# Conformer on one core: weight loads interleaved with modulation vectors, the last three tiles' first taps as diagonal-weight products, and norm roots formed on all partitions

## The chip, the cores and the metric

The kernel runs on 1 core of one Trainium2 chip. The metric is device time in microseconds (us) of one launch; the kernel before took 2624.41 us, the median of 3 runs (2624.28 to 2628.53). The engines are called as the profile calls them: PE does matrix products (PEld its weight loads), DVE vector work, ACT activations and casts, POOL small vector work, and SP issues most of the transfers.

## The reference

The network is a trunk of two layers on one sequence of 256 positions and 2048 channels, all in f32. Layer 0 mixes tokens by a causal Conformer convolution, layer 1 by a Mamba-2 mixer, and each mixer is followed by a squared-ReLU MLP of width 8192. A conditioning vector `c` gives shift, scale and gate vectors for every sub-layer.

```python
sc = jax.nn.silu(c)
mod = (sc @ w_mod[i] + b_mod[i])[:, None, :]
sh1, sc1, g1, sh2, sc2, g2 = jnp.split(mod, 6, axis=-1)
u = rmsnorm(h, norm_mix_g[i]) * (1 + sc1) + sh1
# layer 0: the Conformer convolution
v = u @ w_pw1 + b_pw1
a, gt = jnp.split(v, 2, axis=-1)
v = a * jax.nn.sigmoid(gt)
v = causal_dwconv(v, w_dw, b_dw)            # 31 taps per channel
v = jax.nn.silu(layernorm(v, ln_g, ln_b))
h = h + g1 * (v @ w_pw2 + b_pw2)
u = rmsnorm(h, norm_mlp_g[i]) * (1 + sc2) + sh2
h = h + g2 * sq_relu_mlp(u, w1, w2)
```

The change touches layer 0 up to its MLP, and the root of the norms ahead of both MLPs.

## The kernel before, in words

**Layout.** Activations lie transposed: channels on the 128 partitions, 256 positions along the free axis. The 2048 channels are 16 tiles, in four groups g of four tiles; `h[g]` is one group of the residual.

**Modulation vectors.** One `w_mod` slice of 1 MB gives 128 entries of a vector. A slice is loaded whole and reduced either by DVE (`gemv`, line 255: a product with the broadcast silu(c) in `scb`, summed along the row) or, for the groups in `PE_GROUPS`, by four PE products (line 245), with four more PE products per group (line 269) that turn the row into a column. SC1, SH1 and G1 are scale, shift and gate of the mixer; SC2, SH2 and G2 those of the MLP.

**Transfers.** Every slice and every weight tile is issued on SP's queue, in the order in which the program asks for them (`stream`, line 301): a transfer that waits for its buffer holds all that follow. Weight tiles `w` of 1 MB have three buffers, vectors have two of the kind `wm` and four of the kind `hid`, taken in the ring wm, hid, hid (`self.rings`).

**Opening of layer 0.** The square of `h` is summed tile by tile on DVE (`square_sum`), and the root is formed on two columns and spread back over all partitions (`rstd_cols`, lines 446 to 450, then `spread`, lines 459 and 460). Then the first three 256-column blocks of `w_pw1` (`FIRST = 3`) are multiplied group by group, as each group of the normalised `u` becomes ready (`native`, `vectors`; products on line 591): group g needs its eight vectors SC1 and SH1. SP's order is eight vectors, three weight tiles, eight vectors, three weight tiles, and so on. Group 3 is split into two halves.

**Blocks 3 to 7.** Each remaining block has 16 product instructions per group. Under them ACT makes 24 of the 31 depthwise taps of each channel tile (line 531), DVE the other seven and the additions (lines 539 to 558). `pump` mixes vectors for later stages (the jobs of `EARLY`, then of `LATER`) into the blocks at rates given by tables: `RATE_PW1` inside the blocks, `BETWEEN` before and after the LayerNorm, `RATE_PW2` within the second pointwise product.

**LayerNorm and pw2.** After block 7 come the rest of the pumped vectors, the moments of tiles 0 to 11 (lines 571 and 634), the sums of the last four tiles (line 643), the mean and variance chain (lines 646 to 652), normalisation, silu (line 665), and the split of the result into a high and a low part (lines 427 and 428). Then pw2 runs as fp32r products (line 325) of weights that ACT rounds to a high part `wh` (line 316) and DVE subtracts to a low part `wl` (line 317).

**MLP of layer 0.** The norm root comes again through `rstd_cols` and `spread`. For each group, DVE and ACT form `nrm` (line 478) and the high and low part of `u` (lines 430 and 431), while PE multiplies the first blocks of `w1`. Vectors SC2 and SH2 of the MLP that were not pumped earlier come here as `gemv` on DVE.

Of the kernel before, what the change touches and what calls it, by code (L numbers as in the profile page):

```python
# [15 lines left out]
P = 128  # L16
T = 256
D = 2048
# [21 lines left out]
AHEAD_GLU, AHEAD_CHAIN = 40, 400  # L40
# [6 lines left out]
RATE_PW1 = spread(12, 20)  # L47
BETWEEN = 8, 4
RATE_PW2 = spread(16, 16)
# [5 lines left out]
OPEN = 3  # L55
ACT_TAPS = 24

# [3 lines left out]
PE_GROUPS = {(0, G1, g) for g in range(4)} | {(0, SC2, 0), (0, SH2, 0)}  # L61
# [26 lines left out]
def layout(inp):  # L88
# [26 lines left out]
    for l, s, g in PE_GROUPS:  # L115
        cols = wm[l, :, s, 4 * g:4 * g + 4].reshape(4, 4, P, 512)
        wmt[l, s, 4 * g:4 * g + 4] = cols.transpose(0, 2, 1, 3).reshape(4, P, D)
    return {
        "fg": np.ascontiguousarray(a["final_norm_g"].reshape(1, D)),
# [28 lines left out]
class Trunk:  # L148
# [41 lines left out]
    def prologue(self):  # L190
# [12 lines left out]
        for i in range(4):  # L203
            ps = self.bank(self.mm, "mm")
            nc.tensor.matmul(ps, lhsT=self.ones[:1, :], rhs=row[:, i * 512:(i + 1) * 512], start=True, stop=True)
            nc.scalar.activation(out=scb[:, i * 512:(i + 1) * 512], in_=ps, func=AF.Silu)
# [7 lines left out]
                                compare_op=ALU.is_ge, fill=NEG, base=0, channel_multiplier=-1)  # L214
        self.sel = self.t("bT", [P, T], bufs=1)[:, :P]
# [3 lines left out]
        self.eps = self.const("eps", [P, 1])  # L219
        nc.gpsimd.memset(self.eps, EPS)  # L220
# [215 lines left out]
    def rstd_bcast(self, sums, n):  # L436

        return self.spread(self.rstd_cols(sums, n))
# [46 lines left out]
    def conformer(self):  # L485
        nc, a = self.nc, self.a
        ss = []
        for g in range(4):
            for t in range(4):
                ss = self.square_sum(ss, self.h[g][:, t, :])  # L490
        r = self.t("t2", [P, T], bufs=3)
        nc.scalar.copy(out=r, in_=self.rstd_bcast(ss, D))
# [10 lines left out]
        def vectors(g, t0, t1):  # L503

            for t in range(t0, t1):
                self.gemv(0, SC1, 4 * g + t, halves=g == 3)
                self.gemv(0, SH1, 4 * g + t, halves=g == 3)
# [17 lines left out]
        def conv(ct):  # L525

            vp = vpad[ct % 12]

            def products(p4, k):
                for q in range(4):  # L530
                    nc.scalar.activation(out=p4[:, q, :], in_=vp[:, k + q:k + q + T], func=AF.Identity,  # L531
                                         scale=self.col("w_dw", ct * TAPS + k + q),
                                         bias=self.col("b_dw", ct) if k + q == 0 else 0.0)
# [3 lines left out]
            wide = products(four("wh"), 0)  # L537
# [600 lines left out]
```

## Time and profile before

| | us |
|---|---|
| median of the timed runs | 2624.41 |
| profiled execution, its own time | 2629.66 |
| its span | 2627.8 |
| PE busy in the span | 2528.1 (96%) |
| first product of pw1 (line 591) | 42.79 |
| last product of pw1 | 309.70 |
| last sum of the LayerNorm's moments (line 643) ends | 341.37 |
| first silu (line 665) | 348.41 |
| first product of pw2 (line 325) | 349.85 |
| first product of the MLP of layer 0 | 455.44 |

The timeline gives for each row the start and the length in us, the engine, the line, the operation, the tiles written and read, and in brackets the idle time before it with what ended it. A matmul in f32 (lines 591, 643) leaves two records per instruction. The windows view gives, for stretches of the span, the busy time of each engine with its number of instructions, then the granted PE clock as a share of full speed, the DMA share and the GB/s moved.

### The profile page before, as it was taken

The page shows a single profiled execution, that of the slowest core. Times are in us where ns is not written, and L with a number is a line of the kernel's source. Part 1 is how long each engine was busy: PE and PEld are TensorE (multiplying, and loading weights), DVE is VectorE, ACT ScalarE, POOL GpSimd, SP SyncE. Part 2 cuts the span into 40 slices and gives each one's busy share as a digit, 9 for nine tenths or more (in the row PEclk, how much of TensorE's full clock was granted, in tenths as well). Part 3 has the DMA queues.
Part 4 walks back from the last instruction along what each step waited for, and adds up shares of the span by engine and source line. Part 5 has one row for each costly group of instructions (what it writes and reads, how often), then busy time and mean ns, then how long its engine had stood idle before and what let it go on. Part 6 is the DMA issues. An engine that isn't in the chain of part 4 may idle for free.

```text
span 2627.8 us, 37071 instructions
## 1 busy us (share of the span) xinstructions
PE 2528.1 (96%) x14561; PEld 2188.6 (83%) x14561; DVE 1993.5 (76%) x2663; ACT 1370.0 (52%) x2176; POOL 136.0 (5%) x178
## 2 busy tenths in 40 slices
PE   5889979999999999999999999999999999999998
PEld 3777679988888888888888888888998888888886
DVE  6579798987888889888877777988865565565565
ACT  2089864544444434446777666744444344443443
POOL 1000000000000000000000000000000101101000
PEclk9989989999999999999999999999999999999999
DMA  9855778888888888875555555688665555555554
GB/s 377 358 202 208 312 288 346 314 317 314 306 332 325 319 310 329 306 286 200 188 191 175 178 181 188 238 294 315 238 223 189 193 185 193 192 187 195 183 189 144
DMA packets 92593, 657.43 MB, mean 250 GB/s; under 512 B 10465, under 2 KB 10465, under 8 KB 14465
## 3 DMA queue, kind: packets, MB, share of 16 engines
q1 hardware_dynamic: 88274, 640.73, 66.5%
q0 software_dynamic: 3136, 10.59, 1.4%
q10 hardware_dynamic: 1008, 3.75, 0.4%
q8 instruction: 114, 1.87, 0.3%
q14 instruction: 61, 0.50, 0.1%
HBM read 652.83 MB, written 2.20 MB: 249 GB/s over the span
## 4 chain that ended last, share of the span: by engine, by line
PE 91%; DVE 3%; DMA 3%; ACT 1%; issue 1%; POOL 0%; ACTq 0%; SPq 0%; DVEq 0%
PE mm L325 66%; PE mm L591 8%; PE mm L377 4%; PE mm L376 4%; PE mm L375 4%; DMA hid<-wmT 2%; DVE wl L317 1%; PE mm L245 1%; PE ms L1052 0%; DVE wm L255 0%; PE ms L446 0%; ACT acc L665 0%; PE ms L460 0%; DMA h<-xT 0%; PE ms L1021 0%
## 5 line engine op out<-in xcount | busy, mean ns | idle before, releaser
L325 PE MATMUL mm<-u,wh 128*128 128x512 f32 (+1 forms) x4544 | 1371.8, 364 | 6.8 <-ACT u L427 3.0
L316 ACT CAST wh<-w 128x1024 fp32r<-128x1024 f32 x768 | 806.3, 1051 | 996.3 <-PE mm L325 740.2
L317 DVE TENSOR_TENSOR wl<-w,wh 128x1024 fp32r<-128x1024 f32 x768 | 941.1, 1229 | 454.2 <-ACT wh L316 451.1
L325 PE MATMUL mm<-u,wl 128*128 128x256 f32 x3840 | 1078.6, 282 | 2.1 <-DVE wl L317 2.0
L325 PEld LDWEIGHTS mm<-u,wh 128*128 128x128 f32 x4544 | 812.3, 190 | 148.7 <-issue 3.4
L325 PEld LDWEIGHTS mm<-u,wl 128*128 128x128 f32 x3840 | 730.3, 190 | 7.5 <-DVE wl L317 3.5
L325 PE MATMUL mm<-hid,wh 128*128 128x512 f32 (+1 forms) x1344 | 449.0, 384 | 2.8 <-DVE acc L724 2.8
L325 PE MATMUL mm<-hid,wl 128*128 128x256 f32 x1280 | 358.2, 280 | 0.0
L255 DVE SCALAR_TENSOR_TENSOR wm<-wm,scb 128x2048 f32<-128x2048 f32 x129 | 294.7, 2285 | 2.1 <-DMA wm<-wmT 2.0
L325 PEld LDWEIGHTS mm<-hid,wh 128*128 128x128 f32 x1344 | 247.7, 188 | 56.0 <-DVE acc L724 3.2
L591 PE MATMUL mm<-u,w 128*128 128x256 f32 x1024 | 233.0, 389 | 20.7 <-ACT u L513 20.7
L591 PEld LDWEIGHTS mm<-u,w 128*128 128x128 f32 x1024 | 198.6, 195 | 58.4 <-ACT u L513 21.8
L325 PEld LDWEIGHTS mm<-hid,wl 128*128 128x128 f32 x1280 | 241.9, 189 | 0.4 <-issue 0.2
L377 PE MATMUL mm<-wh,hid 128*128 128x512 f32 x512 | 199.9, 390 | 0.0
L375 PE MATMUL mm<-wh,hid 128*128 128x512 f32 x512 | 199.9, 390 | 0.0
L376 PE MATMUL mm<-wl,hid 128*128 128x512 f32 x512 | 199.5, 390 | 0.0
L531 ACT ACTIVATE taps<-u,par 128x256 f32<-128x256 f32 x384 | 158.2, 502 | 0.6 <-DVE u L522 0.6
L255 DVE SCALAR_TENSOR_TENSOR hid<-hid,scb 128x2048 f32<-128x2048 f32 x39 | 89.1, 2287 | 40.6 <-DMA hid<-wmT 29.7
L377 PEld LDWEIGHTS mm<-wh,hid 128*128 128x128 f32 x512 | 96.1, 188 | 19.7
L375 PEld LDWEIGHTS mm<-wh,hid 128*128 128x128 f32 x512 | 96.2, 188 | 19.6
L376 PEld LDWEIGHTS mm<-wl,hid 128*128 128x128 f32 x512 | 96.1, 188 | 19.6
L278 POOL TENSOR_TENSOR mod<-mod,par 128x4 f32<-128x4 f32 (+1 forms) x50 | 41.0, 821 | 1360.0 <-DVE wm L255 964.0
(209 smaller groups left out, 1586.8 us busy)
## 6 DMA issues: line engine op xcount, KB each, us to landing
w<-w SPq DMA_DIRECT2D x256, 1024.0 KB, 4.9
wm<-wmT SPq DMA_DIRECT2D x137, 1024.0 KB, 7.1
w<-win SPq DMA_DIRECT2D x80, 1024.0 KB, 4.9
hid<-wmT SPq DMA_DIRECT2D x55, 1024.0 KB, 9.6
w<-pw SPq DMA_DIRECT2D x48, 1024.0 KB, 5.0
w<-wout SPq DMA_DIRECT2D x32, 1024.0 KB, 6.8
acc<-ac_d POOLq DMA_DIRECT2D x16, 512.0 KB, 6.7
h<-xT ACTq DMA_DIRECT2D x4, 512.0 KB, 12.8
```

The source lines that it names most:

```text
L245: self.pe = nc.tensor.matmul(self.row_sums[32 * t:32 * t + 32, :], lhsT=self.scol[:, kt:kt + 1].broadcast_to([P, 32]), rhs=w[:, t * 512:(t ...
L255: nc.vector.scalar_tensor_tensor(out=w, in0=w, scalar=1.0, in1=self.scb, op0=ALU.mult, op1=ALU.mult, accum_out=m[:, i:i + 1])
L278: nc.gpsimd.tensor_tensor(out=m, in0=m, in1=self.col("b_mod", (layer * 6 + seg) * NT + 4 * kg + i0, n), op=ALU.add)
L316: nc.scalar.copy(out=wh, in_=w[:, s, :])
L317: nc.vector.tensor_tensor(out=wl, in0=w[:, s, :], in1=wh.bitcast(F32), op=ALU.subtract)
L325: self.pe = self.nc.tensor.matmul(out, lhsT=lhsT, rhs=rhs, skip_group_check=True, **kw).ins
L375: mm(banks[q], lhsT=hi, rhs=wh[:, k, :], start=g == 0 and t == 0, stop=False)
L376: mm(banks[q], lhsT=hi, rhs=wl[:, k, :], start=False, stop=False)
L377: mm(banks[q], lhsT=lo, rhs=wh[:, k, :], start=False, stop=g == 3 and t == 3)
L531: nc.scalar.activation(out=p4[:, q, :], in_=vp[:, k + q:k + q + T], func=AF.Identity, scale=self.col("w_dw", ct * TAPS + k + q), bias=self ...
L591: self.pe = nc.tensor.matmul(o, lhsT=w[:, t, j * P:(j + 1) * P], rhs=u[g][:, t, :], start=g == 0 and t == 0 and j < 2, stop=g == 3 and t == 3,
```

## The change

In the opening, the vector `c` is loaded broadcast to all partitions and put through silu there, `h` comes through SP's queue, and the vectors of the next group are asked for between the three weight tiles of the group before. Squares of `h` are no longer added on DVE: sixteen PE products with a matrix of ones sum them. `rstd_bcast` does the same for the norms of both MLPs, and takes the root and its reciprocal on a 128x256 tile.

`PE_GROUPS` loses the first group of SH2, so that four vectors go from PE to DVE. The rates change: eight instead of twelve vectors in the blocks of pw1, four and six instead of eight and four around the LayerNorm, and a front-loaded `RATE_PW2`.

For the last three channel tiles, the first fifteen of the 31 taps become PE products with diagonal weight matrices, which the host lays out (`diag`, 0.98 MB a tile); ACT makes twelve taps and DVE four. The diagonal matrices lie in three of the `hid` buffers, and from block 7 to the LayerNorm chain vectors use the two `wm` buffers alone. The convolution of the last tile is asked for after the first pumped vectors behind block 7. Normalisation of groups 1 to 3 behind the LayerNorm gets a lower priority than that of group 0.

```diff
-RATE_PW1 = spread(12, 20)
-BETWEEN = 8, 4
-RATE_PW2 = spread(16, 16)
+RATE_PW1 = spread(8, 20)
+BETWEEN = 4, 6
+RATE_PW2 = [2, 1, 1, 1] + spread(13, 12)
+DIAG, PE_TAPS, FEW_TAPS = 3, 15, 12
-PE_GROUPS = {(0, G1, g) for g in range(4)} | {(0, SC2, 0), (0, SH2, 0)}
+PE_GROUPS = {(0, G1, g) for g in range(4)} | {(0, SC2, 0)}
...
-        row = self.b("wm", [1, D], bufs=2)
-        nc.sync.dma_start(out=row, in_=a["crow"])
+        nc.sync.dma_start(out=scb, in_=a["crow"].broadcast_to([P, D]))
-            nc.scalar.dma_start(out=self.h[g], in_=a["xT"][g])
+            nc.sync.dma_start(out=self.h[g], in_=a["xT"][g])
...
     def rstd_bcast(self, sums, n):
-        return self.spread(self.rstd_cols(sums, n))
+        nc = self.nc
+        ps = self.bank(self.ms, "ms")[:, :T]
+        for i, s in enumerate(sums):
+            nc.tensor.matmul(ps, lhsT=self.ones, rhs=s, start=i == 0, stop=i == len(sums) - 1)
+        r = self.t("t2", [P, T], bufs=3)
+        nc.scalar.activation(out=r, in_=ps, func=AF.Sqrt, scale=1.0 / n, bias=self.eps)
+        nc.vector.reciprocal(r, r)
+        return r
...
         for g in range(4):
+            sq = self.b("acc", [P, 4, T], bufs=5)
             for t in range(4):
-                ss = self.square_sum(ss, self.h[g][:, t, :])
-        r = self.t("t2", [P, T], bufs=3)
-        nc.scalar.copy(out=r, in_=self.rstd_bcast(ss, D))
+                nc.scalar.activation(out=sq[:, t, :], in_=self.h[g][:, t, :], func=AF.Square)
+                ss.append(sq[:, t, :])
+        r = self.rstd_bcast(ss, D)
...
+            few = ct >= NT - DIAG
+            k0, k1 = (PE_TAPS, PE_TAPS + FEW_TAPS) if few else (0, ACT_TAPS)
...
+            if few:
+                i = ct - (NT - DIAG)
+                part = (self.bank(self.mm, "mm") if i else self.bank(self.ms, "ms"))[:, :T]
+                with self.tc.issue_after(self.pe):
+                    for k in range(PE_TAPS):
+                        nc.tensor.matmul(part, lhsT=diag[i][:, k, :], rhs=vp[:, k:k + T], start=k == 0,
+                                         stop=k == PE_TAPS - 1)
...
+            if few:
+                nc.vector.tensor_add(wide[:, 0, :], part, wide[:, 0, :])
...
+            vec = lambda n: [self.gemv(0, s, 4 * n[0] + n[1], halves=n[0] == 3) for s in (SC1, SH1)]
+            for t in range(4):
+                vec((0, t))
+            vectors(0, 0, 4)
+            for g in range(3):
+                for i in range(3):
+                    load(i, g)
+                    products(i, g, 0, 4)
+                    if i < 2:
+                        vec((g + 1, i))
+                if g < 2:
+                    for t in (2, 3):
+                        vec((g + 1, t))
+                    vectors(g + 1, 0, 4)
+            vectors(3, 0, 2)
+            for i in range(3):
+                if i:
+                    vec((3, 1 + i))
+                load(i, 3)
+                products(i, 3, 0, 2)
+            vectors(3, 2, 4)
+            for i in range(3):
+                products(i, 3, 2, 4)
...
+            if b == 7:
+                self.rings = ("wm",)
+                diag = []
+                for i in range(DIAG):
+                    diag.append(self.b("hid", [P, PE_TAPS, P]))
+                    self.stream(diag[i], a["diag"][i])
             native([b], glu, pump=pump)
...
         self.pump(BETWEEN[0])
+        close(ct, conv(ct))
+        ct += 1
...
-            for g in range(4):
+        for g in range(4):
+            with self.tc.high_priority(AHEAD_CHAIN if g == 0 else AHEAD_NORM):
...
+        self.rings = ("wm", "hid", "hid")
         with self.tc.issue_after(self.pe):
             self.pump(BETWEEN[1])
```

SP's queue in the opening, from the last of the eight vectors of group 0 on (`hid`, `wm` are vectors, `w` weight tiles); before:

```order
L301 DMA hid_236<-wmT 128x2048
L301 DMA w_58_252<-pw 128x2048
L301 DMA w_59_254<-pw 128x2048
L301 DMA w_60_256<-pw 128x2048
L301 DMA wm_306<-wmT 128x2048
L301 DMA hid_310<-wmT 128x2048
L301 DMA hid_314<-wmT 128x2048
L301 DMA wm_317<-wmT 128x2048
L301 DMA hid_320<-wmT 128x2048
L301 DMA hid_323<-wmT 128x2048
L301 DMA wm_326<-wmT 128x2048
L301 DMA hid_332<-wmT 128x2048
```

and with the change:

```order
L307 DMA hid_203<-wmT 128x2048
L307 DMA w_38_219<-pw 128x2048
L307 DMA wm_237<-wmT 128x2048
L307 DMA hid_241<-wmT 128x2048
L307 DMA w_41_245<-pw 128x2048
L307 DMA hid_263<-wmT 128x2048
L307 DMA wm_266<-wmT 128x2048
L307 DMA w_44_269<-pw 128x2048
L307 DMA hid_287<-wmT 128x2048
L307 DMA hid_290<-wmT 128x2048
L307 DMA wm_293<-wmT 128x2048
L307 DMA hid_299<-wmT 128x2048
```

Two vectors now stand behind the first tile, two behind the second, and four behind the third.

PE behind the last products of block 7 (the first rows; line 245 there is 251 with the change, 643 is 692), before:

```order
L591 MATMUL mm_1640<-u_187,w_260_1707 128x256 x8
L245 MATMUL mm_1751<-wm_1748,scol 32x512 x4
...
L245 MATMUL mm_1751<-wm_1768,scol 32x512 x4
L269 MATMUL mm_1776<-bT_114,t_262_1715 128x1 x4
...
L245 MATMUL mm_1786<-wm_1797,scol 32x512 x4
L245 MATMUL mm_1786<-hid_1803,scol 32x512 x4
...
L571 MATMUL ms_1378<-acc_202,ones 32x256 x4
...
L634 MATMUL mm_1828<-t_281_1826,bT_114 128x512
...
L643 MATMUL mm_1828<-nrm_1969,ones 128x256
L245 MATMUL mm_2057<-hid_2054,scol 32x512 x4
...
L269 MATMUL mm_2082<-bT_114,t_279_1809 128x1 x4
L325 MATMUL mm_2097<-u_1988,wh_2107 128x256
```

and with the change (line 555 is a diagonal-weight product, `hid` its matrices):

```order
L611 MATMUL mm_1584<-u_154,w_236_1645 128x256 x8
...
L251 MATMUL mm_1689<-wm_1700,scol 32x512 x4
L251 MATMUL mm_1689<-wm_1706,scol 32x512 x4
L275 MATMUL mm_1714<-bT_105,t_238_1653 128x1 x4
L555 MATMUL ms_1721<-u_151,hid_1577 128x256 x15
...
L683 MATMUL mm_1774<-t_255_1772,bT_105 128x512
...
L555 MATMUL mm_1776<-u_151,hid_1579 128x256 x15
L555 MATMUL mm_1819<-u_152,hid_1581 128x256 x5
...
L555 MATMUL mm_1819<-u_152,hid_1581 128x256 x10
...
L692 MATMUL mm_1774<-nrm_1860,ones 128x256
L251 MATMUL mm_1948<-wm_1945,scol 32x512 x4
...
L331 MATMUL mm_2000<-u_1879,wh_2027 128x256 x2
```

Four vectors stay ahead of the moments, eight go behind the last sums, and 45 diagonal-weight products stand between them.

DVE in the opening of the MLP of layer 0, ahead of the low parts of the last group of `u` (line 431, 437 with the change), before:

```order
L478 SCALAR_TENSOR_TENSOR nrm_3819<-h_78,mod_3232,ms_3199 128x256
L478 SCALAR_TENSOR_TENSOR nrm_3823<-h_78,mod_3232,ms_3199 128x256
L317 TENSOR_TENSOR wl_3763<-w_525_3756,wh_3762 128x1024
L317 TENSOR_TENSOR wl_3767<-w_525_3756,wh_3766 128x1024
L255 SCALAR_TENSOR_TENSOR wm_3758,mod_3760<-wm_3758,scb 128x2048
L431 SCALAR_TENSOR_TENSOR u_3818<-nrm_3819,mod_3497,u_3818 128x256
L431 SCALAR_TENSOR_TENSOR u_3818<-nrm_3823,mod_3497,u_3818 128x256
L478 SCALAR_TENSOR_TENSOR nrm_3827<-h_78,mod_3232,ms_3199 128x256
L478 SCALAR_TENSOR_TENSOR nrm_3831<-h_78,mod_3232,ms_3199 128x256
```

and with the change:

```order
L491 SCALAR_TENSOR_TENSOR nrm_3745<-h_78,mod_3411,t_422_3117 128x256
L491 SCALAR_TENSOR_TENSOR nrm_3749<-h_78,mod_3411,t_422_3117 128x256
L323 TENSOR_TENSOR wl_3679<-w_493_3672,wh_3678 128x1024
L323 TENSOR_TENSOR wl_3683<-w_493_3672,wh_3682 128x1024
L261 SCALAR_TENSOR_TENSOR hid_3674,mod_3676<-hid_3674,scb 128x2048
L261 SCALAR_TENSOR_TENSOR wm_3734,mod_3676<-wm_3734,scb 128x2048
L261 SCALAR_TENSOR_TENSOR hid_3737,mod_3676<-hid_3737,scb 128x2048
L261 SCALAR_TENSOR_TENSOR hid_3740,mod_3676<-hid_3740,scb 128x2048
L437 SCALAR_TENSOR_TENSOR u_3744<-nrm_3745,mod_3676,u_3744 128x256
L437 SCALAR_TENSOR_TENSOR u_3744<-nrm_3749,mod_3676,u_3744 128x256
L491 SCALAR_TENSOR_TENSOR nrm_3753<-h_78,mod_3411,t_422_3117 128x256
L491 SCALAR_TENSOR_TENSOR nrm_3757<-h_78,mod_3411,t_422_3117 128x256
```

Where one vector (`scb` as a factor) stood between the group's `nrm` and `u`, four stand now; the `nrm` of the other two tiles follows in both.

More of the change, by code (lines that the diff above doesn't have):

```diff
@@ L197, in prologue @@
         nc.gpsimd.memset(self.ones, 1.0)
-        row = self.b("wm", [1, D], bufs=2)
-        nc.sync.dma_start(out=row, in_=a["crow"])
+        nc.sync.dma_start(out=scb, in_=a["crow"].broadcast_to([P, D]))
         nc.scalar.dma_start(out=self.par, in_=a["par"])
         for g in range(4):
-            nc.scalar.dma_start(out=self.h[g], in_=a["xT"][g])
[L203 to L206, printed above, removed]
+            nc.sync.dma_start(out=self.h[g], in_=a["xT"][g])
+        for i in range(2):
+            v = scb[:, i * 1024:(i + 1) * 1024]
+            nc.scalar.activation(out=v, in_=v, func=AF.Silu)
         self.scol = self.const("scol", [P, NT])
```

49 lines of the change are left out of this document (22 added, 27 removed).

## The prediction

> **What bounds the kernel now.** I read the page's busy times and chain first.
>
> ```profile
> PE 2528.1 (96%) x14561; PEld 2188.6 (83%) x14561; DVE 1993.5 (76%) x2663; ACT 1370.0 (52%) x2176; POOL 136.0 (5%) x178
> PE 91%; DVE 3%; DMA 3%; ACT 1%; issue 1%; POOL 0%; ACTq 0%; SPq 0%; DVEq 0%
> ```
>
> PE sets the end. So a change pays where it shortens the time in which PE idles or takes work from PE, and costs where it gives PE work or makes it wait. The timeline of PE shows where it idled (number and cause in brackets):
>
> ```profile
> 42.79 43.46 PE L591 MATMUL mm<-u,w 128*128 128x256 f32 x192 [1.67 <-ACT u L513]
> 94.96 34.31 PE L591 MATMUL mm<-u,w 128*128 128x256 f32 x144 [8.71 <-ACT u L513]
> 139.58 20.37 PE L591 MATMUL mm<-u,w 128*128 128x256 f32 x80 [10.32 <-ACT u L513]
> 319.69 1.94 PE L245 MATMUL mm<-hid,scol 128*32 128x512 f32 x8 [2.66 <-DMA hid<-wmT]
> 339.29 1.22 PE L643 MATMUL mm<-acc,ones 128*128 128x256 f32 x2 [7.77 <-DVE acc L558]
> 349.85 0.78 PE L325 MATMUL mm<-u,wh 128*128 128x256 f32 x3 [2.95 <-ACT u L427]
> ```
>
> There are two places: the opening, up to 152.95 (the last 80 records end at 159.95 and hold 32 of block 3, 7.0 us), and the tail from the last product of pw1 at 309.70 to the full pace of pw2. In the opening ACT's `u` waits for the last vector of its group, so I looked at what the transfers did, in the windows view, and why SP held them, in the waits of SP's queue over the first 160 us:
>
> ```profile
> 0.00:10.00 10.00, 6.86 (x8) 2.49 (x8) 0.00 (x0) 3.07 (x4) 3.02 (x32) 1.00 0.83 322
> 10.00:20.00 10.00, 0.30 (x1) 0.00 (x0) 8.31 (x10) 4.96 (x12) 0.00 (x0) 1.00 1.02 419
> 40.00:50.00 10.00, 8.33 (x29) 6.91 (x30) 8.15 (x10) 2.19 (x5) 0.00 (x0) 1.00 1.02 423
> 60.00:70.00 10.00, 10.00 (x48) 8.81 (x47) 3.98 (x6) 1.82 (x4) 0.20 (x1) 1.00 0.57 215
> 110.00:120.00 10.00, 10.00 (x48) 8.81 (x47) 2.90 (x4) 0.91 (x2) 0.20 (x1) 1.00 0.34 111
> ...
> SPq L301 <- PE mm L591: 85.6, 12, 24.6
> ```
>
> The transfers run full to 50 us, then twice fall to a half and a third, because three weight tiles stand in a row and each needs a buffer that PE still reads; the vectors behind them are held too.
>
> **The change part by part.** *Opening.* With the weight tiles spread, a tile's buffer is asked for only after two more vectors, so SP waits less. Up to the last of the 32 vectors pass 1.05 MB of broadcast `c`, 0.6 MB of parameters, 2.1 MB of `h`, 33.6 MB of vectors and 11 tiles of 1.05 MB, 48.8 MB. The first 10 us carry 3.2 MB; the other 45.6 MB at 0.422 MB/us (between 419 and 423 GB/s) take 108 us, to 118.0. The last vector then needs its landing, two gemvs, whose duration is this row, POOL's addition and `u`:
>
> ```profile
> L255 DVE SCALAR_TENSOR_TENSOR wm<-wm,scb 128x2048 f32<-128x2048 f32 x129 | 294.7, 2285 | 2.1 <-DMA wm<-wmT 2.0
> 302.62 7.15 PE L591 MATMUL mm<-u,w 128*128 128x256 f32 x32
> 309.70 1.06 PE L245 MATMUL mm<-wm,scol 128*32 128x512 f32 x8
> 313.27 1.05 PE L269 MATMUL mm<-bT,t 128*128 128x1 f32 x8
> ```
>
> That is 5.7 us in all, 123.7. Four half groups of products remain (the third tile of group 3 is now loaded last): 16 instructions take 7.0 us, so 14.0, end 137.7. Twice PE's group 2 gives a buffer of `w` free hardly ahead of its tile, for which I add 1.2: end at 139.0 instead of 152.95, **-14.0**. Bounds: -15.2 without that wait, and nothing if SP is held as often as before (second rival). The sixteen square sums move to PE before 42.79, where it has nothing else.
>
> *Blocks 3 to 7.* Four gemvs fewer (four instructions, 0.97 to the next start: 3.9) and one conversion of columns (0.98): **-4.9**. The bound below is nothing, if ACT or DVE set the pace; I take the full sum since each loses taps (36 by ACT, 9 by DVE), and the third rival prices the other. Block 7 thus ends at 309.7 - 18.9 = 290.8.
>
> *Tail.* Times from the end of block 7, with rows of the tail of before, in order of time:
>
> ```profile
> 310.83 0.33 SPq L301 DMA_DIRECT2D wm<-wmT  x1
> 316.00 1.04 PE L245 MATMUL mm<-wm,scol 128*32 128x512 f32 x8
> 326.00 2.07 PE L634 MATMUL mm<-t,bT 128*128 128x512 f32 x2 [0.71 <-ACT t L631]
> 340.31 1.06 PE L643 MATMUL mm<-nrm,ones 128*128 128x256 f32 x2
> 343.96 1.03 ACT L316 CAST wh<-w 128x1024 fp32r<-128x1024 f32 x1
> 347.12 1.28 ACT L665 ACT_TABLE_LOAD   x1
> 348.41 1.09 ACT L665 ACTIVATE acc<-acc,par 128x256 f32<-128x256 f32 x2
> 360.60 0.70 ACT L427 CAST u<-acc 128x256 fp32r<-128x256 f32 x2
> 361.20 2.94 ACT L316 CAST wh<-w 128x1024 fp32r<-128x1024 f32 x3
> 368.33 0.28 PE L325 MATMUL mm<-u,wl 128*128 128x256 f32 x1
> ```
>
> Before, the last sums end at 341.4 (+31.7), the first silu stands at +38.7, the last split at +51.5, and pw2 runs at full pace from 368.15 (+58.45). With the change the four vectors behind block 7 share two buffers, so the third and fourth are issued when PE has used the first and second, and a transfer issued at 310.83 was used at 316.00, 5.2 later: PE waits, and the gemvs and columns end at about +12.8. Then the diagonal products: 15 instructions of 128x256 in f32 are 6.56 us by the 7.0 for 16, 19.7 for the three tiles. With the moments, the spread of 2.07 and the sums (about 0.9 each) between and behind them, the last sum ends at +41.8, 10.1 later. PE's waits of 2.66 and 7.77 are gone, but its own work fills more than their place. Then eight gemvs instead of four, their copies, and two casts stand ahead of the silus: first silu at +52.6, 10.8 behind the sums against 7.0. And SP holds all pw2 weights behind vectors whose `hid` buffers the diagonal products release, so that only one tile is cast ahead of the silus, where before more were (the row at 343.96 is one); from the first silu to full pace 22.8 against 19.75. Sum: 10.1 + 3.8 + 3.0, **+17**. Bounds: +10, if the casts and copies fit between, and +21, if PE goes at half clock, which the windows show after a wait:
>
> ```profile
> 94.90:101.00 6.10, 6.04 (x14) 4.89 (x15) 0.88 (x2) 1.31 (x4) 0.00 (x0) 0.50 1.01 415
> 101.00:107.00 6.00, 6.00 (x29) 5.26 (x29) 4.95 (x5) 0.00 (x0) 0.00 (x0) 1.00 1.01 421
> ```
>
> After 8.71 us of waiting the clock is 0.50 for 6.1 us and half the products pass. I put this cold stretch in the +12.8, in gemvs and columns, and take the diagonal products at full speed, since nothing they need is late. The Trainium skill (TensorE: Matmul & The Clock Gate, Part 1) says that full clock returns after one busy window of 3.4 us and is lost after one idle window of that length; the two rows show a longer return. By the page's figure the tail would come out shorter by an estimated 1 us.
>
> *Opening of the MLP of layer 0.* The four vectors of SH2 that left PE come to DVE, three of them ahead of the last group of `u`. The window up to the first product of group 3 (432 records make three groups) and DVE's rows:
>
> ```profile
> 455.00:509.50 54.50, 53.96 (x434) 53.67 (x435) 0.96 0.84 318
> 503.56 2.29 DVE L255 SCALAR_TENSOR_TENSOR wm<-wm,scb 128x2048 f32<-128x2048 f32 x1
> 505.77 0.88 DVE L431 SCALAR_TENSOR_TENSOR u<-nrm,mod,u 128x256 fp32r<-128x256 f32 x2
> 509.62 0.87 DVE L431 SCALAR_TENSOR_TENSOR u<-nrm,mod,u 128x256 fp32r<-128x256 f32 x2
> ```
>
> PE takes the first low part at 509.5; the first two stand at 506.6 and the other two at 510.5, needed half a block of products later (54.5 / 18 = 3.0), at 512.5. Three gemvs of 2.29 make both 6.9 later: 6.9 less a slack of 2.0, **+4.9**. Bounds: nothing, if DVE waits enough before to take it up, and 6.9 without slack.
>
> *Norm roots.* Before, ACT's root and from there DVE and PE up to `nrm`:
>
> ```profile
> 452.13 0.26 ACT L449 ACTIVATE rcol<-ms,eps 128x2 f32<-128x2 f32 x1
> 454.30 0.87 DVE L478 SCALAR_TENSOR_TENSOR nrm<-h,mod,ms 128x256 f32<-128x256 f32 x2 [1.19 <-PE ms L460]
> 343.54 0.51 ACT L651 ACTIVATE a<-a,eps 128x256 f32<-128x256 f32 x1 [1.28 <-DVE a L650]
> 344.89 1.75 DVE L652 RECIPROCAL a<-a 128x256 f32<-128x256 f32 x1
> ```
>
> From 452.13 to 454.30 is 2.17; the LayerNorm's rows give 0.51 + 1.75 = 2.26 on 256 columns. Three roots: **+0.5**, with the handovers.
>
> Sum: -14.0 - 4.9 + 17 + 4.9 + 0.5 = +3.5 on the profiled execution's own 2629.66 us, 2633.2. That execution lies 5.2 us above the median of the runs, so 2628.
>
> **The rivals.** *The tail is cheaper (2618).* The waits overlap: copies, casts and the eight gemvs run while DVE and ACT do the LayerNorm chain, the tail costs +10, and the gemvs in the MLP's opening cost 2 because DVE's waits there take them up. Then -14.0 - 4.9 + 10 + 2 + 0.5 = -6.4 and 2618. For it: before, PE idles 2.95 ahead of pw2, so ACT and not PE sets that place. Against it: the order of the copies and casts on ACT, ahead of the first silu.
>
> *The opening doesn't fill (2642).* The change doesn't do what it says: SP still stands at a `w` buffer. At the mean of the stretch from 10 to 130 us before,
>
> ```profile
> 10.00:130.00 120.00, 81.16 (x349) 69.76 (x348) 77.52 (x91) 16.57 (x37) 5.54 (x16) 0.96 0.91 371
> ```
>
> 45.6 MB end at 133, the last `u` at 138.6 and the opening at 152.6: nothing gained, +17.5, 2642. It decides from the point where PE frees a buffer of `w` later than the tile that needs it has its turn, about 103 us for the first tile of group 3. Half of it gives 2635. The Trainium skill (DMA: Bandwidth & Descriptors, Where 436 GB/s comes from) goes further: it calls 358 GB/s the limit that binds from HBM, and by it the opening would end near 157, an estimate; the windows of 419 to 423 GB/s speak against it, so it adds nothing to this rival's chance.
>
> *ACT or DVE becomes the bound (2636).* In this stretch of the blocks both are nearly full:
>
> ```profile
> 160.00:200.00 40.00, 40.00 (x197) 31.57 (x196) 39.14 (x61) 39.67 (x100) 0.00 (x0) 1.00 0.59 214
> ```
>
> If the blocks can't go faster than ACT's taps, the 4.9 is lost, the sums of tiles 11 and 12 come late, PE waits ahead of the second diagonal tile and does the rest of these products at 0.50: 3 more, +8 over the forecast, 2636. It decides once ACT has more to do in such a stretch than its reserve, 0.3 of 40 us. Against it: the 45 taps that both lose, of which ACT's 36 alone are more than a tile's 24.
>
> **How the numbers follow.** A measurement of this kernel can tell about 0.2%, 5.2 us, from no change. The forecast, 2628 with its own range of 2622 to 2631, gets 0.36; the cheap tail 0.30; the unfilled opening 0.20; ACT or DVE 0.14. So faster 0.30, no change 0.36, slower 0.34. The range holds 2618 and 2636 and, leaving about one in ten on each side, goes from 2612 to 2641.
>
> **What would show it.** Right: in the first 115 us of the changed profile no window under 380 GB/s, the last products of the opening near 139; the last product of block 7 near 291; 5 us of waiting before the third vector behind it; last sum near 333, first silu near 343, pw2 at full pace near 366; one wait of 4 to 5 us of PE on DVE's `u` in the MLP's opening. Wrong: windows of 200 GB/s in the opening, a clock of 0.50 in the diagonal products, products of the diagonal far from 0.44 us, or an MLP opening without that wait.

## The result: slower by 0.8%, and where it went

The changed kernel takes 2646.97 us (median of 4 runs, 2646.03 to 2648.51), the kernel before 2624.73 us beside it: a ratio of 1.0082 with a 95% interval of 1.0065 to 1.0100, some 22 us. The forecast was 2628, the range 2612 to 2641. The profiled execution took 2647.28 us with a span of 2645.5, 17.7 more than the span before.

The page of the changed kernel: its span, busy times and chain.

```profile
span 2645.5 us, 37019 instructions
PE 2543.8 (96%) x14587; PEld 2208.8 (83%) x14587; DVE 1990.0 (75%) x2634; ACT 1357.0 (51%) x2137; POOL 126.2 (5%) x178
PE 91%; DVE 3%; DMA 3%; ACT 1%; issue 1%; POOL 0%; ACTq 0%; DVEq 0%; SPq 0%
```

PE is busy for 15.7 us more, near the 17.7 by which the span grew; the shares of the chain read as before. A page like this says only that PE got more to do, or did some of it more slowly. The timeline of PE, at the places where it waited (in brackets), says where:

```profile
125.87 29.58 PE L611 MATMUL mm<-u,w 128*128 128x256 f32 x128 [3.42 <-ACT u L524]
298.58 1.94 PE L251 MATMUL mm<-wm,scol 128*32 128x512 f32 x8 [4.03 <-DMA wm<-wmT]
305.21 9.66 PE L555 MATMUL ms<-u,hid 128*128 128x256 f32 x30
335.69 0.70 PE L692 MATMUL mm<-acc,ones 128*128 128x256 f32 x2 [2.16 <-DVE acc L580]
452.42 0.70 PE L447 MATMUL ms<-ssum,ones 128*128 128x256 f32 x2 [1.69 <-DVE ssum L480]
460.21 1.91 PE L331 MATMUL mm<-u,wh 128*128 128x256 f32 x5 [5.00 <-ACT u L436]
519.20 1.08 PE L331 MATMUL mm<-u,wh 128*128 128x256 f32 x4 [4.64 <-ACT wh L322]
1982.02 1.12 PE L836 MATMUL ms<-ident,h 128*128 128x128 f32 x4 [4.86 <-ACT wm L837]
```

PE's last wait of the opening ends at 125.87 instead of 139.58, with four half groups of products left instead of three: the new order of the loads works. But the last four of these rows are places that stood still less, or not at all, before: the sums ahead of the first MLP, its opening at 519.20, and the transposes in the last MLP at 1982.02. I cut both executions at marks that both have, and give each stretch its length in us (block 3 begins 14.0 before the end of the row at 125.87, whose last 64 records are its first two groups; pw1 ends at 292.6 in the changed kernel; the tail and pw2 are parted at the start of the first of pw2's last four updates of `h`):

| stretch | before | after | difference |
|---|---|---|---|
| opening of layer 0 (up to the first product of block 3) | 152.95 | 141.45 | -11.5 |
| blocks 3 to 7, up to the end of pw1 | 156.75 | 151.2 | -5.6 |
| end of pw1 to the first of the last four updates of `h` by pw2 | 137.1 | 156.1 | +18.9 |
| from there to the first product of the first MLP | 8.6 | 11.5 | +2.9 |
| to the first sum into `acc`: the first MLP's opening | 116.4 | 124.2 | +7.8 |
| to the last sum into `acc` ahead of the last MLP | 1224.8 | 1224.8 | 0 |
| to the end | 831.2 | 836.3 | +5.1 |

The sum is +17.6. Before, the first product of the first MLP had waited 1.25 us where it now waits 5.00:

```profile
455.44 1.90 PE L325 MATMUL mm<-u,wh 128*128 128x256 f32 x5 [1.25 <-ACT u L430]
```

The opening's windows (columns: time, busy us of PE, PEld, DVE, ACT and POOL, granted PE clock, DMA share, GB/s) show the full transfers that were forecast:

```profile
10.00:20.00 10.00, 9.20 (x32) 7.48 (x32) 4.75 (x5) 6.65 (x18) 0.00 (x0) 1.00 1.03 426
60.00:70.00 10.00, 7.06 (x26) 5.64 (x25) 8.27 (x11) 1.81 (x4) 0.79 (x4) 0.83 1.01 422
110.00:120.00 10.00, 10.00 (x48) 8.82 (x47) 5.85 (x5) 0.00 (x0) 0.00 (x0) 1.00 0.99 405
```

Where 215 and 111 GB/s were moved before, 422 and 405 are now. In the first MLP's opening, DVE and ACT of the changed kernel show who is late:

```profile
508.06 2.28 DVE L261 SCALAR_TENSOR_TENSOR hid<-hid,scb 128x2048 f32<-128x2048 f32 x1
514.70 2.29 DVE L261 SCALAR_TENSOR_TENSOR hid<-hid,scb 128x2048 f32<-128x2048 f32 x1
517.30 0.91 ACT L436 ACTIVATE u<-nrm,mod 128x256 fp32r<-128x256 f32 x2 [10.41 <-POOL mod L284]
518.12 1.98 ACT L322 CAST wh<-w 128x1024 fp32r<-128x1024 f32 x2
...
519.00:525.00 6.00, 5.37 (x32) 5.07 (x33) 6.00 (x9) 3.65 (x6) 0.00 (x0) 0.72 0.15 61
```

Four vectors run in a row on DVE from 508.06 to 516.91 (the first and the last are shown). ACT stands 10.41 us at the high part of `u`, which needs the last of them, and the next casts of weights come behind it in ACT's queue. The product that waits is the first of the last group: it needs both this `u`, written from 517.30 on, and `wh`, cast from 518.12 on. So most of its wait is the late vector's own, and the cast behind it adds the last 1.3 us (from 517.8, when the first half of the row at 517.30 is done, to 519.1, when the first cast is). PE then runs at a mean clock of 0.72 for 6 us. The last MLP shows a similar form: ACT's copy of transposed rows needs a `wm` buffer that a late vector still holds.

```profile
1979.05 2.29 DVE L261 SCALAR_TENSOR_TENSOR wm<-wm,scb 128x2048 f32<-128x2048 f32 x1
1981.38 0.58 ACT L837 COPY wm<-ms 128x512 f32<-128x512 f32 x1 [4.69 <-DVE wm L261]
1982.00:1986.00 4.00, 2.23 (x8) 1.44 (x8) 2.30 (x2) 0.61 (x2) 0.00 (x0) 0.50 1.02 424
```

The wait of 4.86 us at 1982.02 is the first of three there, 7.2 us together. Before, the copy at that place waited 1.80 us and PE 1.55, the first of three waits of 2.6 us together:

```profile
1967.23 0.59 ACT L786 COPY wm<-ms 128x512 f32<-128x512 f32 x1 [1.80 <-DVE wm L255]
1967.87 0.66 PE L785 MATMUL ms<-ident,h 128*128 128x128 f32 x4 [1.55 <-ACT wm L786]
```

### The profile page after: what moved, and what is told of

The parts are those of the page before. It is cut to its first block, busy times and chain, and to the rows that moved or that the text cites. A ratio compares the mean times of both kernels' runs of the same rounds, so it can differ in the third digit from the quotient of the medians.

```text
span 2645.5 us, 37019 instructions
## 1 busy us (share of the span) xinstructions
PE 2543.8 (96%) x14587; PEld 2208.8 (83%) x14587; DVE 1990.0 (75%) x2634; ACT 1357.0 (51%) x2137; POOL 126.2 (5%) x178
## 3 DMA queue, kind: packets, MB, share of 16 engines
q1 hardware_dynamic: 89424, 646.81, 65.2%
## 4 chain that ended last, share of the span: by engine, by line
PE 91%; DVE 3%; DMA 3%; ACT 1%; issue 1%; POOL 0%; ACTq 0%; DVEq 0%; SPq 0%
PE mm L331 67%; PE mm L611 6%; PE mm L383 4%; PE mm L382 4%; PE mm L381 4%; DMA wm<-wmT 1%; DMA hid<-wmT 1%; DVE hid L261 1%; DVE wm L261 1%; DVE wl L323 1%; PE mm L251 1%; PE ms L1103 1%; PE ms L447 1%; PE mm L555 0%; PE ms L555 0%
## 5 line engine op out<-in xcount | busy, mean ns | idle before, releaser
L544 ACT ACTIVATE taps<-u,par 128x256 f32<-128x256 f32 x348 | 143.2, 501 | 0.6 <-DVE u L533 0.6
L383 PEld LDWEIGHTS mm<-wh,hid 128*128 128x128 f32 x512 | 96.2, 188 | 19.7
```

The source lines that it names most:

```text
L383: mm(banks[q], lhsT=lo, rhs=wh[:, k, :], start=False, stop=g == 3 and t == 3)
```

## The experiments

The **theory** after the comparison: the *vector budget*. `PE_GROUPS` and the rates leave 36 instead of 40 vectors done before the first MLP, and four go from PE to DVE; the waits in both MLPs come from these, and the diagonal products lengthen the tail. The **rivals**: the new norm roots, with a reciprocal of 1.75 us on DVE, are behind the waits; or the taps would end that much later without the diagonal products. The kernel before took 2624.7 us in the session of the result and 2628.4 to 2629.0 in the others, so all comparisons are ratios to it in the same session; 0.001 is 2.6 us. The result's own session has only four runs of the kernel before, so part of this gap may be chance: by medians alone, each difference to the change is 2.5 to 4 us smaller than the ratios say.

### Four parts apart

**The budget mended in pw2** (changed kernel):

```diff
-RATE_PW2 = [2, 1, 1, 1] + spread(13, 12)
+RATE_PW2 = [2, 1, 1, 1] + spread(17, 12)
```

> The changed kernel, with four vectors more in the second pointwise product (22 instead of 18), so that as many are done before the MLP of layer 0 as in the kernel before (40 of 48). Theory (the vector budget: four fewer vectors done early is what makes PE wait 4.6 us with a cold clock in the MLP's opening and 7.2 us with a cold clock at the transposes of the last MLP): 12 to 14 us faster than the changed kernel, 2633 to 2635, both waits gone. Rival (the norm roots and their order on DVE make these waits): no change, 2647. A third way: DVE, busy 70 of 79 us in that product, can't take 9.2 us more and the time comes back there: 2640.

Measured: ratio 1.0055 (1.0043 to 1.0067), 7 us less than the change, 4 by the medians; the intervals just touch. The first MLP's opening falls from 124.2 to 116.6 and the end from 836.3 to 830.4: both waits are gone, as the budget theory has it. But from the first silu to the first MLP it takes 123.1 instead of 112.8, so most comes back in pw2: the third way of the expectation.

**The old roots in all later norms** (changed kernel; the opening keeps the new one):

```diff
     def rstd_bcast(self, sums, n):
+        if len(sums) < 16:
+            return self.spread(self.rstd_cols(sums, n))
```

> The changed kernel, with the norm roots of both MLPs and of the Mamba mixer in the old form (two columns, spread back); the opening keeps the new form. Vector budget theory: only what stands at the roots themselves changes, 0 to 3 us faster, 2644 to 2647. Rival (the roots are at the bottom of the waits in the MLP openings): 8 us or more faster, under 2639.

Measured: 1.0069 (1.0057 to 1.0081), 3 us less with overlapping intervals. The first MLP's opening stays at 125.8, the end at 836.6. The first MLP still comes 11.3 us after the updates of `h` (11.5 with the new roots, 8.6 before). The roots are not behind the waits; that rival falls.

**The opening alone**, first try: the changed kernel with the taps, budget and roots of before. Beyond what the expectation says, the normalisation's groups had their priority set one by one.

```diff
-            for g in range(4):
+        for g in range(4):
+            with self.tc.high_priority(AHEAD_CHAIN):
```

> The kernel before with the new opening alone (order of the loads, broadcast of c, square sums on PE); vectors, rates, taps, roots of the MLPs and priorities as before. If the 13 us that the changed kernel gains up to the end of the opening are kept by all that follows: 2611 to 2613. If ACT and DVE, nearly full in the blocks, or the transfers give it back: 2618 to 2625.

Measured: 0.9976 (0.9966 to 0.9986); the median of 2623.56 lies in the second case, the ratio at its better end. PE waited 6.96 us for the first silus' results where it had waited 2.95, which led to the second try below.

**No diagonal products** (changed kernel):

```diff
-DIAG, PE_TAPS, FEW_TAPS = 3, 15, 12
+DIAG, PE_TAPS, FEW_TAPS = 0, 15, 12
...
             if b == 7:
-                self.rings = ("wm",)
...
         self.pump(BETWEEN[0])
-        close(ct, conv(ct))
-        ct += 1
```

> The changed kernel without the diagonal-weight products: ACT makes 24 and DVE 7 taps of the last three tiles again, the vectors use all buffers, and the last tile's convolution stands where it did. If the diagonal products are what lengthens the tail (19.7 us of PE and two waits for vectors in two buffers): the tail shortens by 10 to 15 us, 2632 to 2637. If ACT and DVE would end their taps that much later, so that the products pay for themselves: 2645 to 2655.

The loads of the matrices go too, vectors use all buffers again, and the last tile's convolution stands where it did before. Measured: 1.0006 (0.9997 to 1.0014), 20 us less than the change, 16 by the medians, more than was expected. Its timeline of PE at the last sums:

```profile
310.83 1.22 PE L679 MATMUL mm<-acc,ones 128*128 128x256 f32 x2 [10.77 <-DVE acc L575]
320.02 1.22 PE L679 MATMUL mm<-acc,ones 128*128 128x256 f32 x2 [7.12 <-DVE acc L575]
```

PE waits 17.9 us for taps, yet the sums are done near 322, where with the products they end near 337. From the end of pw1 to the first silu the tail takes 41.9 instead of 55.1 (39.0 before). The products gave PE 19.7 us of work, 3.1 more of it at half clock, and two waits for vectors (4.03 and 1.11), for a wait of 17.9. What the restriction to two vector buffers costs apart from the products is not separated here.

### Each part on the kernel before

**The opening alone, second try**: the kernel before, with the new prologue, square sums, first norm root and load order of the first three blocks, and nothing else.

> The kernel before, line for line, with the new opening alone. The earlier run of this kind also formed the priorities of the LayerNorm's groups one by one, and PE then waited 6.96 and 3.03 us for the silus' results where the kernel before waits 2.95 and 1.08. If that was where part of the opening's 12 us went: 2613 to 2617 against 2624.4 of before, a ratio of 0.995 to 0.997. If the blocks or the transfers gave it back: a ratio of 0.9976 as there.

Measured: 0.9948 (0.9935 to 0.9960), 13.6 us faster than before, the fastest kernel of this study. The page's span and PE's last wait of the opening:

```profile
span 2612.7 us, 37057 instructions
125.54 22.67 PE L590 MATMUL mm<-u,w 128*128 128x256 f32 x96 [3.05 <-ACT u L514]
```

All stretches behind pw1 have their old length (39.2, 107.0, 116.3 and 831.1 us), so the opening's gain is kept whole. That is just past the good end of the first case, and the rest of the change costs 33 to 35 us on top (by the medians and by the ratios).

**Budget and moved group on the new opening**:

```diff
-RATE_PW1 = spread(12, 20)
-BETWEEN = 8, 4
-RATE_PW2 = spread(16, 16)
+RATE_PW1 = spread(8, 20)
+BETWEEN = 4, 6
+RATE_PW2 = [2, 1, 1, 1] + spread(13, 12)
-PE_GROUPS = {(0, G1, g) for g in range(4)} | {(0, SC2, 0), (0, SH2, 0)}
+PE_GROUPS = {(0, G1, g) for g in range(4)} | {(0, SC2, 0)}
```

> The kernel before with the new opening and, of the rest, the changed vector rates and the group that moves from PE to DVE alone. Vector budget theory: the blocks gain 4, the opening of the first MLP loses 7.8 and the last MLP 5, so 7 to 10 us slower than the opening alone, ratio 0.9975 to 0.9988. If the waits in the MLPs need the diagonal products or the new roots: ratio 0.993 to 0.995.

Measured: 1.0022 (1.0014 to 1.0031), 19 us slower than the opening alone, double what was expected. Pw1 ends 6.6 earlier, but the first MLP's opening takes 126.6 and the end 836.6, and pw2 4.3 more. This alone would have turned the opening's gain into a loss.

**The count alone** (new opening; the group stays on PE):

```diff
-RATE_PW1 = spread(12, 20)
+RATE_PW1 = spread(8, 20)
```

> The kernel before with the new opening, and eight instead of twelve vectors in the blocks of the first pointwise product, nothing else: the group of SH2 stays on PE, but 36 instead of 40 vectors are done before the MLP. The changed rates and the moved group together cost 19 us on this base (ratio 1.0022 against 0.9948). If the count of vectors done early is the cause: 12 to 19 us slower than the opening alone, ratio 0.9995 to 1.002. If the move of the group from PE to DVE is: within 4 us of it, 0.994 to 0.9965.

Measured: 0.9988 (0.9979 to 0.9997), 10.5 us slower. Opening of the first MLP 126.8, end 837.3, pw2 as before. Its timeline of PE:

```profile
502.52 1.23 PE L323 MATMUL mm<-u,wh 128*128 128x256 f32 x4 [6.13 <-ACT wh L314]
1965.55 0.66 PE L805 MATMUL ms<-ident,h 128*128 128x128 f32 x4 [4.43 <-ACT wm L806]
```

One number in a table makes both waits, 1460 us apart.

**The group with the count kept** (new opening; 40 vectors before the MLP, four more of them on DVE, and four moved from the blocks to pw2):

```diff
-PE_GROUPS = {(0, G1, g) for g in range(4)} | {(0, SC2, 0), (0, SH2, 0)}
-RATE_PW1 = spread(12, 20)
-RATE_PW2 = spread(16, 16)
+PE_GROUPS = {(0, G1, g) for g in range(4)} | {(0, SC2, 0)}
+RATE_PW1 = spread(8, 20)
+RATE_PW2 = spread(20, 16)
```

> The kernel before with the new opening, the group of SH2 moved to DVE, eight vectors in the blocks and twenty in the second pointwise product: 40 vectors are done before the MLP as in the kernel before, four more of them by DVE. If the count is the cause: the MLP's opening and the last MLP as fast as before (116 and 831 us), and a loss of 4 to 8 us where DVE gets four more vectors, ratio 0.9965 to 0.9985. If the move of the group is: ratio 1.000 or above.

Measured: 0.9992 (0.9982 to 1.0001), 11.6 us slower than the opening alone. The end is 829.7, the first MLP's opening 119.0, so the count does make these waits; but pw2 grows from 107.0 to 118.0. The windows view of pw2's full stretch in this run and with the opening alone:

```profile
346.00:441.00 95.00, 88.86 (x700) 88.08 (x700) 85.81 (x95) 32.32 (x42) 12.94 (x12) 0.95 0.92 365
```

```profile
352.00:437.00 85.00, 83.46 (x696) 83.46 (x697) 77.31 (x88) 33.14 (x43) 5.54 (x9) 1.00 0.94 363
```

The same products (700 and 696 records) take 95 instead of 85 us; DVE's busy time grows by 8.5, four gemvs being 9.2. PE's longest wait in this stretch shows how a vector reaches PE:

```profile
408.52 2.28 DVE L253 SCALAR_TENSOR_TENSOR hid<-hid,scb 128x2048 f32<-128x2048 f32 x1
411.57 0.42 ACT L468 ACTIVATE sq<-h 128x256 f32<-128x256 f32 x1 [2.52 <-DVE h L727]
412.98 1.44 PE L323 MATMUL mm<-u,wh 128*128 128x256 f32 x5 [3.46 <-ACT wh L314]
```

A vector on DVE delays an update of `h`, ACT's square of it waits, the cast of the next weights comes behind the square, and PE waits 3.46 us for the cast. The mean clock over the stretch is 0.95 instead of 1.00. The count thus came out just under its 12 to 19, the group above its 4 to 8. Both edits take four vectors out of the blocks, so their costs can't simply be added; but the stretches part them. The missing four make the waits in both MLPs, four more vectors on DVE make pw2 longer, and neither alone is the cause of the 19 us.

### Whether the costs can be had back one by one

**The count mended late** (changed kernel):

```diff
-RATE_MLP = spread(80, 116) + [0] * 50
+RATE_MLP = spread(84, 116) + [0] * 50
```

> The changed kernel with 84 instead of 80 vectors pumped during the MLP of layer 0 and the Mamba projections. Vector budget theory: the last MLP's transposes no longer wait for four late vectors, 4 to 6 us faster than the changed kernel, ratio 1.006 to 1.0067; the opening of the first MLP stays as slow as it is. Rival: no change, 1.0082.

Measured: 1.0054 (1.0040 to 1.0067), 7 us less than the change. The end takes 828.0 instead of 836.3 and the first MLP's opening stays at 124.1, as expected; the profile shows 7.8 more between them, which the timed runs don't bear out, so the size is open. (This stretch lies between 1221.2 and 1228.4 in all other profiles of this study.)

**The budget of before on PE** (the kernel without diagonal products):

```diff
-BETWEEN = 4, 6
-RATE_PW2 = [2, 1, 1, 1] + spread(13, 12)
+BETWEEN = 8, 8
+RATE_PW2 = spread(16, 16)
-PE_GROUPS = {(0, G1, g) for g in range(4)} | {(0, SC2, 0)}
+PE_GROUPS = {(0, G1, g) for g in range(4)} | {(0, SC2, 0), (0, SH2, 0)}
```

> The changed kernel without diagonal-weight products, with the first group of SH2 back on PE, eight vectors before and eight behind the moments, sixteen in the second pointwise product: as many vectors are done before the MLP as in the kernel before, and the four that return to PE go where PE waited 10.8 and 7.1 us for the taps. Vector budget theory: the MLP's opening and the last MLP give back 7.8 and 5 us, the tail costs 2 to 3 more, so 10 us faster than the run without diagonal products (ratio 1.0006), 0.996 to 0.998. Rival (the waits in the MLPs come from the roots or the order on DVE): ratio 1.000 to 1.002.

Measured: 0.9995 (0.9986 to 1.0004), only 3 us faster than without this edit, with intervals that overlap, against 10 expected. The MLPs gave back what was said (116.8 and 831.8), but pw2 took 117.5 instead of 111.9:

```profile
347.62 2.07 PE L326 MATMUL mm<-u,wh 128*128 128x256 f32 x8 [11.64 <-ACT wh L317]
```

With eight vectors ahead of pw2's weights in SP's queue, PE waits 11.64 us for the second cast. A vector has to stand somewhere, and each place has its price.

**The diagonal products with the budget of before** (changed kernel; the group of SH2 is on PE again):

```diff
-RATE_PW1 = spread(8, 20)
-BETWEEN = 4, 6
-RATE_PW2 = [2, 1, 1, 1] + spread(13, 12)
+RATE_PW1 = spread(12, 20)
+BETWEEN = 4, 8
+RATE_PW2 = spread(16, 16)
```

> The changed kernel with the vector budget of before (group of SH2 on PE, twelve in the blocks, four and eight around the LayerNorm, sixteen in the second pointwise product); diagonal products, two vector buffers, roots and priorities as changed. If budget and diagonal products cost independently: 1.0082 less 0.0074, ratio 1.000 to 1.002. If the diagonal products already make the same place late, so that the costs overlap: 1.004 or above.

Measured: 1.0048 (1.0036 to 1.0060), the second case by its number. The MLPs are mended (116.7 and 831.4), while the tail stays at 54.0, the blocks take 5.7 us more, and pw2 takes 117.3 with a wait of 10.69 us for a cast:

```profile
364.36 2.08 PE L331 MATMUL mm<-u,wh 128*128 128x256 f32 x8 [10.69 <-ACT wh L322]
```

The run before has the same wait (11.64) without any diagonal product; both put eight vectors ahead of pw2's weights. So this wait belongs to the place of the vectors, and that budget and diagonal products make the same place late is not shown.

### Diagonal products where PE waits

**One tile instead of three** (changed kernel; matrices behind block 7, all vector buffers in use, place of the last tile's convolution as before):

```diff
-DIAG, PE_TAPS, FEW_TAPS = 3, 15, 12
+DIAG, PE_TAPS, FEW_TAPS = 1, 15, 12
```

> The changed kernel with diagonal-weight products for the last tile alone, its matrices loaded behind block 7, all vector buffers in use. Without diagonal products PE waits 10.8 and 7.1 us for the taps of the last four tiles, so 6.6 us of products fit under a wait, and ACT and DVE lose 12 and 3 taps. Theory (the products pay only as far as PE would wait anyway): 2 to 5 us faster than without them, ratio 0.9985 to 1.000. If their loads and the wait for their result cost more: 1.0006 or above.

Measured: 0.9986 (0.9978 to 0.9995), 5 us faster than none, 25 faster than three. PE's waits at the last sums shrink to 4.33 and 1.09:

```profile
310.75 1.22 PE L686 MATMUL mm<-acc,ones 128*128 128x256 f32 x2 [4.33 <-DVE acc L580]
313.92 1.22 PE L686 MATMUL mm<-acc,ones 128*128 128x256 f32 x2 [1.09 <-DVE acc L580]
```

The tail falls from 41.9 to 35.2.

**One tile on the new opening** (kernel before with the opening alone; matrices behind the eight vectors):

> The kernel before with the new opening, and diagonal-weight products for the last tile alone, its matrices loaded behind the eight vectors that follow block 7. With the opening alone PE waits 7.8 us for the taps of the last tiles. Theory (the products pay where PE would wait anyway): the last sums come 4 to 6 us earlier, ratio 0.9925 to 0.9935, faster than either kernel. If the 5 us load or the products themselves come late: 0.9948 as without them, or above.

Measured: 0.9969 (0.9956 to 0.9981), 5 us *slower* than the opening alone, with intervals that just touch; the 0.9925 to 0.9935 that the theory expected are excluded. PE's wait of 7.80 shrinks to 2.16, but the tail only from 39.2 to 37.9, since the products themselves stand in it, and pw2 takes 2.8 more (PE waits 3.65 us there for a low part of the weights).

```profile
324.62 1.22 PE L684 MATMUL mm<-acc,ones 128*128 128x256 f32 x2 [2.16 <-DVE acc L576]
342.12 0.58 PE L329 MATMUL mm<-u,wl 128*128 128x256 f32 x1 [3.65 <-DVE wl L321]
```

**Two tiles on the new opening**:

> As with the products for the last tile alone, but for the last two. PE gets 6.6 us more, of which at most 2 lie under a wait, and two loads stand behind the vectors. Theory: no better than one tile and 2 to 5 us slower, ratio 0.993 to 0.995. If ACT's and DVE's taps were still what ends the tail: 2 to 4 us faster than one tile.

Measured: 0.9981 (0.9970 to 0.9992), 3 us slower than one, with intervals that overlap, and 9 slower than none; the tail is 45.7. A second tile doesn't pay, as expected; the level is off since one tile was.

**The priorities alone on the new opening**:

> The kernel before with the new opening and, of the rest, the changed priorities of the normalisation behind the LayerNorm alone. If they are what makes the stretch from the first silu to the MLP 5 us longer in every run that has them (107.0 before, 112 with them): 4 to 7 us slower than the opening alone, ratio 0.9965 to 0.9975. If that stretch grows for another reason: 0.9948.

Measured: 0.9965 (0.9953 to 0.9976), 4.5 us slower than the opening alone, with intervals that overlap. The expected ratio came, but not at the place: the stretch from the first silu to the MLP is 108.2 against 107.0. Whether the priorities cost anything stays open.

## Why the prediction was wrong, point by point

**Opening.** Right in kind, 2.5 us too good in this profile: -11.5 instead of -14.0. The transfers run at 405 to 426 GB/s from 10 to 120 us, and the rival of the unfilled opening is refuted by these windows. The Trainium skill (DMA: Bandwidth & Descriptors, Where 436 GB/s comes from) states a limit of some 358 GB/s for transfers from HBM; this trace lies above it. The last `u` came at 125.9 instead of 123.7, and the four half groups behind it took 15.6 us instead of the 14.0 of the sum. In seven of the sixteen kernels with this opening they took 13.9, so that part is no fault of the sum (see the last section).

**Blocks 3 to 7.** -5.6 against -4.9. ACT and DVE did not become the bound; that rival falls too.

**Tail.** +18.9 against +17. The two waits for vectors in two buffers are there (4.03 and 1.11), the last sum ends at 336.8 (forecast 333), the first silu stands at 347.4 (343). The bet that the diagonal products run at full speed was lost for the first tile: 30 records took 9.66 us, 6.56 at full clock. PE's granted clock was 0.50 from the end of the first of the two waits, at 298.6, to 311:

```profile
298.60:311.00 12.40, 11.29 (x38) 6.73 (x39) 5.66 (x10) 5.90 (x15) 0.40 (x2) 0.50 0.61 234
```

The cheap tail is refuted. The 3.0 behind the first silu came out right (2.9 up to the updates of `h`), but the reason given, the `hid` buffers that the matrices hold, is not borne out: without diagonal products that stretch is 4.6 longer than before. So in this part the number is as much luck as reasoning.

**Norm roots.** +0.5 was nearly right for the roots (with the old ones the first MLP comes 0.2 us earlier), but the first MLP came 2.9 later. The step costed the root's own operations and not what stands ahead of it: a vector of 2.28 us that the changed order put on DVE just before the sum of squares.

```profile
449.74 2.28 DVE L261 SCALAR_TENSOR_TENSOR hid<-hid,scb 128x2048 f32<-128x2048 f32 x1
451.94 0.42 DVE L480 TENSOR_TENSOR ssum<-ssum,sq 128x256 f32<-128x256 f32 x1
```

**Opening of the first MLP.** +7.8 against +4.9, 0.9 above the step's own upper bound. The wait itself was sized well: 4.64 us. What the step left out stands behind the wait: from the product that waited to the first sum into `acc` it takes 65.2 us, where before it took 62.5, and the mean clock over the first 6 of them is 0.72.

**The step that failed.** The sum followed the four vectors that are missing early only to the first MLP. For the last MLP it put nothing, without a reason, and none of the rivals was "the missing vectors are still missing later". The runs showed +5.1 us there, with PE waiting 4.86 us on a buffer that a late vector held; the run with the count alone shows both waits from one edit, and the runs with 40 early vectors or 84 late ones do not have the second. The terms that the sum did have were each a little too good, but for the blocks. Of the 14 us between forecast (+3.5) and profile (+17.6), the last MLP is 5.1, the first MLP's opening 2.9, the sums ahead of it 2.4, the opening 2.5 and the tail 1.9, less 0.7 in the blocks. In the tail and in the first MLP it is largely PE's low clock behind a wait that had been priced: 3.1 us in the first tile's products, 2.7 behind the wait in the MLP.

**The medians** lie 22 us apart where the two profiles lie 17.7 apart; the forecast was made on the profiled execution, 5.2 above the median of before, and the changed kernel's profiled execution stands only 0.3 above its own. The other 4.6 us come from there; no step of the sum is behind them.

## What to carry to other kernels

When a change moves background work from one stage to later ones, follow the backlog to every place that drains it, however far: four vectors fewer early made PE wait in the next MLP and again 1460 us later, for the late result itself, for casts queued behind it and for a buffer. Filling a wait with other work pays only up to the wait's length, product time and clock included; one diagonal tile under a wait of 17.9 us won 5 us and under a wait of 7.8 won nothing, while three, with the vectors held to two buffers, lost some 16 to 20. To a wait, add the slow products behind it. Take a bundle apart before it is kept or dropped: here one part was worth 13.6 us and the rest cost 33 to 35.

## What the runs showed of the hardware

The same opening did not run at the same clock in every kernel that has it. Behind PE's last wait of the opening stand 64 records of products. In the sixteen kernels with this opening they took 13.92 us in seven, 15.60 in six and 16.6 to 16.9 in three. The length of the wait does not decide it: waits of 2.21 and of 4.21 us both led to 15.60. The windows from 126 to 152 us with one diagonal tile (a wait of 2.96 before it) and with the changed priorities (3.20):

```profile
126.00:152.00 26.00, 26.00 (x125) 21.91 (x124) 15.54 (x23) 20.91 (x52) 0.00 (x0) 1.00 0.61 232
```

```profile
126.00:152.00 26.00, 25.05 (x105) 20.52 (x106) 10.78 (x18) 17.50 (x42) 0.20 (x1) 0.87 0.45 164
```

One kept a clock of 1.00, the other fell to 0.87, and the last products of pw1 began at 295.5 and 300.4; with the opening alone at 297.6, with two tiles at 297.8. So a single profile of one kernel can't tell differences under some 5 us in this stretch. The Trainium skill (TensorE: Matmul & The Clock Gate, Part 1) calls the window that decides free-running and the number of slow products variable from run to run; the spread from 13.92 to 16.9 us agrees with it.
